# Moving gate products between attention and memory steps, with shared scaling, halved projections and split memory gates

## The chip, the cores and the metric

The kernel runs on one core of a Trainium2 chip. The metric is the device time of one execution in microseconds (us). Before the change it is 2273.91 us, the median of three runs (2273.75 to 2274.84). TensorE (PE in the rows) multiplies matrices into PSUM, which has eight banks of 128 x 512 fp32; VectorE (DVE), ScalarE (ACT) and GpSimd (POOL) do everything else; SyncE's queue (SP) issues most loads.

## The reference, cut to what matters

Two layers run over 256 latent tokens and 256 context tokens of width 1024, all in fp32: a half-step SwiGLU, three parallel token mixers, another half-step SwiGLU. The change is in the mixers alone:

```python
y_a = windowed_attention(qa, ka, va, ka_c, va_c, attn_sink)   # A: 8 heads, softmax with a sink
y_b = dense_attention(qb, concat(kb_c, kb), concat(vb_c, vb)) # B: 8 heads, normalised q and k
y_m, y_m_c = mlstm_mixer((qm, km, vm, om, gm), ...)           # C: bidirectional gated memory
...
z = einsum('btnw,nwd->btnd', stack([y_a, y_b, y_m], -2), w_branch)
g = sigmoid(gate_logits.reshape(..., 3, 1024))                # gate_logits = h @ w_in[gate columns]
return sum(g * z, axis=-2) @ w_out
```

In the second (last) layer only latent tokens are needed behind the keys and values, so queries, gates and merge there work on 256 tokens instead of 512.

## The kernel before

A product of fp32 values is made of three fp32r products, high x high, high x low and low x high (`mm3`, L192 to L196). Weights come as units of 128 x 1024 values (512 KB): SP loads one into a "raw" tile (L153, four of them), ACT rounds it to its high part (L163), DVE subtracts to get the low part (L164). A list of tasks, each with the units that it needs, is run in order (`run_tasks`, L168), and units are loaded and split a few tasks ahead. `weave(a, b)` spreads list b evenly through list a. Below the tasks, the framework's planner fixes each engine's order and hands out buffers of a ring as they come free, roughly in the order of the source, so that instructions of neighbouring tasks mix.

`mixer_tasks` (L830) lays out one layer's mixers in this order:

- Projections of branch A's queries, of values and keys; then the first of branch B's query projection `qb` (four tasks `tok_tasks`, L695: each multiplies two of the eight chunks of the inner dimension for all blocks of 128 tokens, 512 columns wide, so that one PSUM bank for each token block, four in all, is held from the first task to the last). The memory values `vm` are made in the same way. In the last layer `qb` is done ahead of the attention.
- Branch A's attention steps, the first half of `att` (16 steps in layer 0, 8 in layer 1), woven with `side`: the memory gates, the rest of `qb`, `vm`, and the queries' transposes; and with `pre_[0]`, gate products of branch 0. A gate product is 24 matmuls of 128 x W (W is 512 in layer 0, 256 in layer 1) into one bank (`gate`, L1299); `ahead` (L1306) copies it with ACT into half of a raw tile and, for each pair, writes it to memory, from where a unit "pre" brings it back for the merge.
- Branch B's steps and the last of A's (19 steps in layer 0, 11 in layer 1), woven with eight convolution tasks, each of which starts with such a product.
- Silu, then the memory steps (`mlstm_steps`), woven with the merge of branch 0 (`mrg[0]`) and gate products of branch 1 (`pre_[1]`); then the projection `om` woven with the merge of branch 1; `put_y2`, which transposes and splits the memory's result, three tasks into the rest of it; then the merge of branch 2 and the output projection.

`PRE = 8, 4, 0` and `PRE_L = 4, 4, 0` say how many of the eight gate products of each branch are made ahead in layer 0 and in layer 1. The others are made inside the merge task `mk` (L1316) itself, which multiplies the branch's result with its weights (12 matmuls), applies the sigmoid and adds up. For a pair that was made ahead, one sigmoid in place covers both halves of the loaded raw tile (L1328).

One attention step i takes two heads: scores into two banks (L1012 to L1015), row maximum (L1016), exponential with row sum (L1030), reciprocal (L1039), then POOL multiplies each head's probabilities with it in turn (L1042). Two steps later the probabilities are transposed into one or two banks (L1054) and split (L1056, through L189 and L190), and a step after that multiplied with the values (L1069, L1071).

The memory gates (`mgate_steps`, L1100) are three tasks: log-sigmoid; `rows`, which transposes them to rows and runs on DVE four scans (L1142), one long scan (L1144) and eleven more row operations (L1146 to L1153) in one task; and `cols`.

## Time and profile before

| | before |
|---|---|
| median of three runs | 2273.91 us |
| the profiled execution | 2271.84 us, of which the span is 2270.1 us |
| busy: TensorE, weight loads | 2195.6 us (97%), 1837.6 us (81%) |
| busy: DVE, ACT, POOL | 1545.9 us (68%), 984.6 us (43%), 133.0 us (6%) |
| mean granted TensorE clock | 0.992 |
| chain that ended last, by engine | PE 84%, DVE 8%, ACT 3%, DMA 2%, issue 2% |
| DMA | 331.36 MB, mean 146 GB/s |

TensorE is nearly always busy; the other engines have room on average, and so have the transfers. Layer 0's mixers run from about 440 to 950 us of the span, layer 1's from about 1750 to 2060 us. The two attention halves lie at 480 to 590 and 590 to 703 us in layer 0, at 1778 to 1840 and 1840 to 1903 us in layer 1; the memory steps at 715 to 781 and 1914 to 1967 us. A matmul's end is modelled, so that successive matmuls overlap in the rows; start times tell their pace.

### The profile page before, as it was taken

The page shows a single profiled execution, that of the slowest core. Times are in us where ns is not written, and L with a number is a line of the kernel's source. Part 1 is how long each engine was busy: PE and PEld are TensorE (multiplying, and loading weights), DVE is VectorE, ACT ScalarE, POOL GpSimd, SP SyncE. Part 2 cuts the span into 40 slices and gives each one's busy share as a digit, 9 for nine tenths or more (in the row PEclk, how much of TensorE's full clock was granted, in tenths as well). Part 3 has the DMA queues.
Part 4 walks back from the last instruction along what each step waited for, and adds up shares of the span by engine and source line. Part 5 has one row for each costly group of instructions (what it writes and reads, how often), then busy time and mean ns, then how long its engine had stood idle before and what let it go on. Part 6 is the DMA issues. An engine that isn't in the chain of part 4 may idle for free.

```text
span 2270.1 us, 30607 instructions
## 1 busy us (share of the span) xinstructions
PE 2195.6 (97%) x11666; PEld 1837.6 (81%) x11666; DVE 1545.9 (68%) x2756; ACT 984.6 (43%) x1569; POOL 133.0 (6%) x100
## 2 busy tenths in 40 slices
PE   6999999998999999999999999999999989998998
PEld 4877777787777888888878788777778878997997
DVE  3987775877678664654444378778849787786556
ACT  3322223554588533542222253222226488655444
POOL 0000000013241000000000000000000142000000
PEclk9999999999999999999999999999999999998999
DMA  7665564422213333434433336665634123565554
GB/s 282 214 196 186 165 199 149 125 81 76 94 38 82 119 119 136 142 115 135 129 114 127 103 107 204 195 195 178 223 116 159 57 89 96 167 228 172 189 186 153
DMA packets 126402, 331.36 MB, mean 146 GB/s; under 512 B 12712, under 2 KB 26088, under 8 KB 125488
## 3 DMA queue, kind: packets, MB, share of 16 engines
q1 hardware_dynamic: 111664, 314.02, 43.0%
q10 hardware_dynamic: 14592, 15.40, 2.2%
q8 instruction: 91, 1.49, 0.3%
q14 instruction: 55, 0.45, 0.1%
HBM read 320.91 MB, written 8.47 MB: 145 GB/s over the span
## 4 chain that ended last, share of the span: by engine, by line
PE 84%; DVE 8%; ACT 3%; DMA 2%; issue 2%; POOL 0%; ACTq 0%; POOLq 0%; SPq 0%; DVEq 0%
PE ps L194 26%; PE ps L195 26%; PE ps L196 26%; PE ps L1243 1%; DVE lo L164 1%; DVE sm L1016 1%; ACT t L1030 1%; PE ps L1212 1%; ACT hi L163 1%; PE ps L366 1%; PE ps L1054 1%; PE ps L468 1%; DVE t L190 0%; DVE slot L959 0%; DMA raw<-in_w_gu_dram 0%
## 5 line engine op out<-in xcount | busy, mean ns | idle before, releaser
L163 ACT ACTIVATE hi<-raw 128x1024 fp32r<-128x1024 f32 (+1 forms) x444 | 457.0, 1032 | 766.8 <-PE ps L195 274.7
L194 PE MATMUL ps<-slot,hi 128*128 128x512 f32 (+1 forms) x2232 | 780.5, 351 | 7.7 <-ACT slot L189 5.3
L195 PE MATMUL ps<-slot,hi 128*128 128x512 f32 (+1 forms) x2232 | 776.9, 349 | 0.9 <-DVE slot L190 0.7
L196 PE MATMUL ps<-slot,lo 128*128 128x512 f32 (+1 forms) x2232 | 776.6, 348 | 0.0
L164 DVE TENSOR_TENSOR lo<-raw,hi 128x1024 fp32r<-128x1024 f32 (+1 forms) x444 | 527.1, 1190 | 245.2 <-ACT hi L163 240.7
L194 PEld LDWEIGHTS ps<-slot,hi 128*128 128x128 f32 x2232 | 421.2, 190 | 77.5 <-ACT slot L189 6.6
L195 PEld LDWEIGHTS ps<-slot,hi 128*128 128x128 f32 x2232 | 422.5, 189 | 57.4 <-DVE slot L190 1.7
L196 PEld LDWEIGHTS ps<-slot,lo 128*128 128x128 f32 x2232 | 421.9, 189 | 57.9
L194 PE MATMUL ps<-hi,slot 128*128 128x512 f32 (+2 forms) x1048 | 400.6, 382 | 1.8 <-ACT slot L189 1.1
L196 PE MATMUL ps<-hi,slot 128*128 128x512 f32 (+2 forms) x1048 | 399.5, 382 | 0.0
L195 PE MATMUL ps<-lo,slot 128*128 128x512 f32 (+2 forms) x1048 | 399.5, 381 | 0.0
L358 DVE SCALAR_TENSOR_TENSOR t<-raw,sc,t 128x1024 f32<-128x1024 f32 x224 | 280.5, 1281 | 128.8 <-DMA raw<-in_w_ada_dram 128.5
L1042 POOL TENSOR_SCALAR t<-t,sm 128x512 f32<-128x512 f32 (+1 forms) x96 | 132.9, 1396 | 1767.1 <-DVE sm L1039 1675.7
L194 PEld LDWEIGHTS ps<-hi,slot 128*128 128x128 f32 x1048 | 197.5, 188 | 46.2 <-issue 5.7
L196 PEld LDWEIGHTS ps<-hi,slot 128*128 128x128 f32 x1048 | 197.0, 188 | 39.3
L195 PEld LDWEIGHTS ps<-lo,slot 128*128 128x128 f32 x1048 | 197.3, 188 | 38.8 <-issue 0.2
L189 ACT ACTIVATE slot<-t 128x512 fp32r<-128x512 f32 (+1 forms) x138 | 80.7, 594 | 185.4 <-DVE t L606 160.2
L606 DVE TENSOR_TENSOR t<-ps,t 128x512 f32<-128x512 f32 (+1 forms) x88 | 54.7, 622 | 89.1 <-PE ps L196 87.8
L190 DVE TENSOR_TENSOR slot<-t,slot 128x512 fp32r<-128x512 f32 (+1 forms) x138 | 87.6, 644 | 4.4 <-ACT slot L189 4.1
L1016 DVE TENSOR_REDUCE sm<-ps 128x1 f32<-128x512 f32 (+1 forms) x96 | 54.4, 593 | 22.2 <-PE ps L1015 21.5
L1054 PE MATMUL ps<-ident,t 128*128 128x128 f32 x320 | 47.7, 282 | 18.6 <-POOL t L1042 8.4
L1054 PEld LDWEIGHTS ps<-ident,t 128*128 128x128 f32 x320 | 37.5, 143 | 28.5 <-POOL t L1042 17.3
(198 smaller groups left out, 1670.6 us busy)
## 6 DMA issues: line engine op xcount, KB each, us to landing
raw<-in_w_gu_dram SPq DMA_DIRECT2D x176, 512.0 KB
raw<-in_w_ada_dram SPq DMA_DIRECT2D x128, 512.0 KB
raw<-in_w_down_dram SPq DMA_DIRECT2D x92, 512.0 KB
raw<-in_w_fm_dram SPq DMA_DIRECT2D x64, 512.0 KB
raw<-in_w_br_dram SPq DMA_DIRECT2D x24, 512.0 KB
raw<-in_w_out_dram SPq DMA_DIRECT2D x24, 512.0 KB
slot<-in_w_ada_dram SPq DMA_DIRECT2D x16, 512.0 KB
raw<-in_w_down_dram SPq DMA_DIRECT2D x20, 256.0 KB
```

The lines of the kernel that those rows point to most:

```text
L163: self.nc.scalar.activation(out=hi, in_=raw, func=AF.Copy)
L164: self.nc.vector.tensor_tensor(out=lo, in0=raw, in1=hi.bitcast(F32), op=ALU.subtract)
L189: self.nc.scalar.activation(out=hi, in_=src, func=AF.Copy)
L190: self.nc.vector.tensor_tensor(out=lo, in0=src, in1=hi.bitcast(F32), op=ALU.subtract)
L194: mm(out, lh, rh, start=start, stop=False, **kw)
L195: mm(out, lh, rl, start=False, stop=False, **kw)
L196: mm(out, ll, rh, start=False, stop=stop, **kw)
L358: v.scalar_tensor_tensor(out=acc, in0=units[0], scalar=c, in1=acc, op0=ALU.mult, op1=ALU.add)
L606: nc.vector.tensor_tensor(out=hid[:, :W], in0=ps[:, :W], in1=hid[:, :W], op=ALU.mult)
L1016: v.tensor_reduce(out=mx[:, e:e + 1], in_=ps[:, :nkey], axis=AX.X, op=ALU.max)
L1042: nc.gpsimd.tensor_scalar(out=t[:, :nkey], in0=t[:, :nkey], scalar1=r[:, e:e + 1], scalar2=None, op0=ALU.mult)
L1054: nc.tensor.transpose(pt[:, n * P:(n + 1) * P], e[n % 2][:, kb * P:(kb + 1) * P], self.ident)
```

## The change

Five things change together; what is computed stays the same.

1. All eight gate products of branches 0 and 1 are made ahead in both layers, those of branch 0 woven with branch A's steps, the first `PRE = 4` of branch 1 woven with the convolutions between branch B's steps, the other four in the memory steps. Of branch 2 the first `HELD = 2` stay in PSUM until their merge tasks; they stand behind the merge of branch 1, and `put_y2` comes right behind them.
2. Each merge task applies its own sigmoid into a new tile, ahead of its products, also where the logits were read back.
3. `qb` and `vm` become `half_tasks`: each unit has four of the eight inner chunks for half of the columns, so two tasks finish 256 columns for all token blocks, two blocks in one bank. The weights are laid out on the host so that a unit is one run of 4 KB for each partition.
4. The scaling of the probabilities is shared: POOL keeps the first head; the second goes to ACT in branch A and to DVE in branch B.
5. `rows` is cut into `rows`, `scans` and `decays`, and the first four gate tasks are woven with what is left of `qb`.

```diff
-PRE = 8, 4, 0
-PRE_L = 4, 4, 0
+PRE = 4
+HELD = 2
...
+    def half_tasks(self, l, name, tbs, ms, evac):
...
+        def mk(h, g):
+            def fn(units):
+                u = units[0]
+                for tb in tbs:
+                    if g == 0 and tb % 2 == 0:
+                        ds[h, tb // 2] = self.psum().rearrange("p (b c) -> p b c", b=2)
+                    ps = ds[h, tb // 2][:, tb % 2, :]
+                    for x in range(4):
+                        lh, ll = ms["hi"][g][:, x, tb * P:(tb + 1) * P], ms["lo"][g][:, x, tb * P:(tb + 1) * P]
+
+                        self.mm3(ps, lh, ll, u[0][:, x, :], u[1][:, x, :], g == x == tb % 2 == 0, g == 1 and x == 3,
+                                 skip_group_check=True)
+                    if g:
+                        evac(tb, h, ps)
+            return ([("half", l, name, h, g)], fn)
+
+        return [mk(h, g) for h in range(2) for g in range(2)]
...
-        side = gates[:1] + qb[:1] + gates[1:2] + qb[1:] + vm_[nv:va] + gates[2:] + vm_[va:vb] + qcols(1) + vm_[vb:]
+        side = weave(gates[:4], qb) + vm_[nv:va] + gates[4:] + vm_[va:vb] + qcols(1) + vm_[vb:]
         na = 4 * len(qtb)
-        out += weave(att[:na], weave(side, pre_[0])) + weave(att[na:], conv)
+        out += weave(att[:na], weave(side, pre_[0])) + weave(att[na:], weave(conv, pre_[1][:PRE]))
         out += self.silu_task(R, need_ctx)
         mem = self.mlstm_steps(R, qs)
-        out += mem[:1] + self.split_y(R, 0, W) + weave(weave(mrg[0], pre_[1]), mem[1:])
+        out += mem[:1] + self.split_y(R, 0, W) + weave(weave(mrg[0], pre_[1][PRE:]), mem[1:])
         out += self.split_y(R, 1, W)
-        out += weave(self.tok_tasks(l, "om", 512, 2, qtb, ms, om), mrg[1][:np_[1]])
-        out += mrg[1][np_[1]:np_[1] + 3] + [([], put_y2)] + mrg[1][np_[1] + 3:]
+        out += weave(self.tok_tasks(l, "om", 512, 2, qtb, ms, om), mrg[1][:2])
+        out += mrg[1][2:] + pre_[2] + [([], put_y2)]
         out += mrg[2]
...
             for e in range(2):
-                t = E[i][e]
-                nc.gpsimd.tensor_scalar(out=t[:, :nkey], in0=t[:, :nkey], scalar1=r[:, e:e + 1], scalar2=None,
-                                        op0=ALU.mult)
+                t = E[i][e][:, :nkey]
+                if e and x == 0:
+                    nc.scalar.activation(out=t, in_=t, func=AF.Copy, scale=r[:, e:e + 1])
+                else:
+                    (v if e else nc.gpsimd).tensor_scalar(out=t, in0=t, scalar1=r[:, e:e + 1], scalar2=None, op0=ALU.mult)
...
-            b_r, m_r = RW[:, 2, :], RW[:, 3, :]
-            i_r, f_r = RW[:, 0, :], RW[:, 1, :]
+            R["RW"] = RW
+
+        def scans(_):
+            RW = R["RW"]
+            i_r, f_r, b_r, m_r = (RW[:, q, :] for q in range(4))
...
+        def decays(_):
...
-        return [([], logsig), ([], rows), ([], cols)]
+        return [([], logsig), ([], rows), ([], scans), ([], decays), ([], cols)]
...
+        def held(j):
+            def fn(units):
+                st[j] = gate(units[0])
             return ([("fm", l, 8 + 8 * n + j)], fn)
...
-                if j >= npre:
-                    pg = gate(units.pop(0))
-                elif j % 2 == 0:
-                    st["g"] = units.pop(0).rearrange("p (a b) -> p a b", a=2)
-                    nc.scalar.activation(out=st["g"], in_=st["g"], func=AF.Sigmoid)
+                if n == 2:
+                    pg = gate(units.pop(0)) if j >= HELD else st.pop(j)
+                else:
+                    if j % 2 == 0:
+                        st["g"] = units.pop(0).rearrange("p (a b) -> p a b", a=2)
+                    pg = st["g"][:, j % 2, :]
+                g = self.t512()[:, :W]
+                nc.scalar.activation(out=g, in_=pg, func=AF.Sigmoid)
```

The row operations behind the halved `qb` (`q_rows`, L749) and the copies behind the halved `vm` work on 256 columns each, twice as often.

## Rows read from the trace of the kernel before

**Rows 1.** The page, busy time (share of the span) and instructions of an engine

```profile
PE 2195.6 (97%) x11666; PEld 1837.6 (81%) x11666; DVE 1545.9 (68%) x2756; ACT 984.6 (43%) x1569; POOL 133.0 (6%) x100
```

**Rows 2.** Stretches: length; PE, PEld, DVE, ACT, POOL busy; clock, DMA share, GB/s

```profile
480.00:590.00 110.00, 104.11 (x570) 85.18 (x569) 83.12 (x217) 57.59 (x127) 33.57 (x24) 1.00 0.19 64
590.00:703.00 113.00, 102.58 (x559) 85.70 (x558) 77.77 (x174) 80.63 (x157) 48.22 (x40) 0.98 0.28 84
1778.00:1840.00 62.00, 55.06 (x346) 45.63 (x344) 49.79 (x127) 33.44 (x73) 19.57 (x13) 0.97 0.19 64
1840.00:1903.00 63.00, 56.36 (x376) 49.91 (x375) 49.28 (x99) 52.10 (x90) 31.50 (x20) 0.97 0.22 73
715.00:781.00 66.00, 66.00 (x371) 57.59 (x370) 50.94 (x221) 46.08 (x91) 0.00 (x0) 1.00 0.28 89
1914.00:1967.00 53.00, 53.00 (x431) 52.09 (x431) 43.68 (x146) 46.56 (x89) 0.00 (x0) 1.00 0.41 135
1967.00:1999.00 32.00, 31.47 (x219) 28.92 (x219) 23.97 (x61) 15.01 (x19) 0.00 (x0) 1.00 0.68 223
```

**Rows 3.** TensorE's waits, 480 to 703 us: us in total, times, longest

```profile
PE ps L1054 <- POOL t L1042: 6.0, 8, 1.2
PE ps L1054 <- DVE t L190: 4.2, 2, 3.2
PE ps L1069 <- ACT t L1030: 2.0, 1, 2.0
...
PE ps L1012 <- ACT t L1030: 0.7, 1, 0.7
```

**Rows 4.** The same view, 1778 to 1903 us

```profile
PE ps L1054 <- DVE t L190: 2.9, 3, 1.2
PE ps L1054 <- POOL t L1042: 2.4, 3, 1.2
PE ps L1069 <- DVE t L190: 2.2, 2, 1.7
```

**Rows 5.** Timeline around 514 to 521 us: start us, length us, instruction, idle before it

```profile
514.66 1.35 DVE L1142 TENSOR_TENSOR_SCAN slot<-ones,slot 8x128 f32<-8x128 f32 x4
...
520.94 0.33 PE L1054 MATMUL ps<-ident,t 128*128 128x128 f32 x1 [3.16 <-DVE t L190]
```

**Rows 6.** Timeline of POOL, one step's pair of heads

```profile
618.52 3.10 POOL L1042 TENSOR_SCALAR t<-t,sm 128x512 f32<-128x512 f32 x2 [6.69 <-DVE sm L1039]
```

**Rows 7.** Groups by line and form: busy us, mean ns | idle before, releasers

```profile
L1042 POOL TENSOR_SCALAR t<-t,sm 128x512 f32<-128x512 f32 x64 | 102.7, 1616 | 1698.9 <-DVE sm L1039 1648.0 <-ACT t L189 18.1 <-ACT sm L1036 13.3
...
L451 DVE TENSOR_SCALAR t<-slot,sm 128x1024 f32<-128x1024 f32 x12 | 9.0, 753 | 0.4
...
L1341 ACT ACTIVATE t<-ps 128x512 f32<-128x512 f32 x12 | 7.0, 581 | 0.0
...
L163 ACT ACTIVATE hi<-raw 128x1024 fp32r<-128x1024 f32 x416 | 439.3, 1058 | 730.8 <-PE ps L195 266.4 <-PE ps L196 166.9 <-issue 154.2
...
L164 DVE TENSOR_TENSOR lo<-raw,hi 128x1024 fp32r<-128x1024 f32 x416 | 507.8, 1223 | 227.6 <-ACT hi L163 223.1 <-PE ps L196 1.4
...
L164 DVE TENSOR_TENSOR lo<-raw,hi 128x512 fp32r<-128x512 f32 x20 | 13.8, 689 | 16.4 <-ACT hi L163 16.4
```

**Rows 8.** Timeline of TensorE where the width of its matmuls changes

```profile
1914.05 0.40 PE L196 MATMUL ps<-slot,lo 128*128 128x512 f32 x1
1914.28 0.28 PE L194 MATMUL ps<-slot,hi 128*128 128x256 f32 x1
1914.40 0.28 PE L195 MATMUL ps<-slot,hi 128*128 128x256 f32 x1
```

**Rows 9.** Timeline of ACT, first and last of seven table loads, 1935 to 1962 us

```profile
1935.18 1.28 ACT L1341 ACT_TABLE_LOAD   x1
1936.47 0.39 ACT L1341 ACTIVATE t<-ps 128x256 f32<-128x256 f32 x1
...
1961.21 1.28 ACT L1341 ACT_TABLE_LOAD   x1
```

More of the change, by code (lines that the diff above doesn't have):

```diff
@@ L127, in unit_src @@
             return src.rearrange("(k p) c -> p k c", p=P), (len(ks), n), True
+        if kind == "half":
+            _, l, name, h, g = key
+            return a["w_" + name][l, h, g], (4, 256), True
         if kind == "fm":
@@ L909, in mixer_tasks @@
         kk_ = self.tok_tasks(l, "kk", 256, 4, range(4), ms, kk)
-        vm_ = self.tok_tasks(l, "vm", 512, 2, range(4), ms, vm)
+        vm_ = self.half_tasks(l, "vm", range(4), ms, vm)
         if need_ctx:
@@ L1144, in rows @@
             v.tensor_tensor_scan(out=m_r, data0=f_r, data1=i_r, initial=0.0, op0=ALU.add, op1=ALU.max)
+        def decays(_):
+            RW = R.pop("RW")
+            i_r, f_r, b_r, m_r = (RW[:, q, :] for q in range(4))
             KR = self.slot([8, 14, P])
@@ L1336, in fn @@
                              R[f"yl{n}"][:, k, :W], k == 0, k == 3)
-                if j < npre:
-                    g = st["g"][:, j % 2, :]
-                else:
-                    g = self.t512()[:, :W]
-                    nc.scalar.activation(out=g, in_=pg, func=AF.Sigmoid)
                 u = R["u"][j // 4][:, j % 4, :]
@@ L1353, in mk @@
             return (keys, fn)
-        return [ahead(j) for j in range(npre)], [mk(j) for j in range(8)]
+        first = [held(j) for j in range(HELD)] if n == 2 else [ahead(j) for j in range(8)]
+        return first, [mk(j) for j in range(8)]
 def weave(a, b, head=0, tail=0):
@@ L1446, in _layout @@
     a["w_qa"] = c(w[:, :, C_QA + qcols])
-    a["w_qb"] = c(w[:, :, C_QB + qcols])
+    halves = lambda m: c(m.reshape(2, 2, 4, P, 2, 256).transpose(0, 4, 1, 3, 2, 5))
+    a["w_qb"] = halves(w[:, :, C_QB + qcols])
     a["w_kk"] = c(np.concatenate([w[:, :, C_KA:C_KA + 128], w[:, :, C_KB:C_KB + 128]], axis=2))
```

47 lines of the change are left out of this document (26 added, 21 removed).

## The prediction

> **What bounds the kernel now.** I read the page's busy times first. TensorE is busy for 2195.6 of 2270.1 us [rows 1], so only its own stream can move the time: either its idle time shrinks, or its work changes. The change adds and removes almost no products, so the question is where TensorE idles, and whether the changed order fills those holes or opens others. The second view is the table of stretches [rows 2]. Its first four rows are the two attention halves of layer 0 and of layer 1: TensorE is missing 110.00-104.11=5.9, 113.00-102.58=10.4, 62.00-55.06=6.9 and 63.00-56.36=6.6 us there, 29.9 us together. In the memory steps of both layers, the next two rows, it is missing nothing, and in the start of layer 1's merge, the last row, 0.5 us. So what can be won lies in the attention, and what can be lost lies in stretches that are full today.
>
> Two things make a hole dearer than its idle time. Matmuls of 512 columns start 0.23 us apart while each is drawn 0.40 us long [rows 8], so the drawn end covers about 0.16 us of each hole. And the granted clock averages 0.98, 0.97 and 0.97 in three of the four stretches [rows 2], that is 0.02x113+0.03x62+0.03x63=6 us of clock, lost in falls to the lower of its two levels (1.2 instead of 2.4 GHz); part of each fall lies in holes, so I count 4 us of it as TensorE time. The view of waits has about 34 of them in these stretches, 5.4 us at 0.16. The ceiling of any gain is therefore about 29.9+5.4+4=39 us, 1.7%.
>
> The third view, who TensorE waited for, splits the 29.9. In layer 0: POOL's probability scaling L1042, 6.0 us in 8 waits; DVE's L190, 4.2 us; and the exponentials L1030 (four rows from 2.0 down to 0.7, 5.2 us together), which is PSUM not yet free [rows 3]. In layer 1: DVE's L190 2.9+2.2, POOL 2.4 [rows 4]. The rest, some 7 us, is scattered.
>
> **The change, part by part.**
>
> *Scaling shared.* POOL scales both heads of a step now, one after the other: 3.10 us for a pair [rows 6]. Afterwards the second head goes to ACT in branch A and to DVE in branch B. The trace has no DVE scaling of 512 columns from SBUF; one of 1024 took 0.753 [rows 7], so half of that, 0.38, and all of it bound the price, and I take 0.4, since a shorter operation cannot be near the full one. ACT's copy of 512 I take from the sigmoid of that size, 0.58 [rows 7]. So the transposes, which wait for both heads, can start about 1.5 us earlier in a 512-column step. The added load is 16x0.4=6 us on DVE in layer 0's branch B, busy there for 77.77 of 113, and 16x0.58=9 us on ACT in branch A, busy for 57.59 of 110 [rows 2]: beside TensorE's work in both. ACT keeps its order, so a scaling that waits for DVE's reciprocal holds the exponentials and weight splits queued behind it, and through them PSUM banks; with half of ACT free in branch A I price that at nothing (up to a reciprocal's delay of some 0.5 us a step, 12 us, if that cover is gone). Of the 8.4 us of POOL waits I take 6.7 as won (0 to 8.4).
>
> POOL's mean for 512 columns is 1616 ns [rows 7], above half of the undisturbed pair in [rows 6]: it slows at times. The Trainium skill (GPSIMD Engine Reference, Key points) says that POOL and DVE share their SBUF interfaces and contend when DVE runs in a two-port mode or with two SBUF inputs; by it the new DVE scaling would run against POOL's half. The trace agrees in that the mean exceeds the pair's half; were POOL's single scaling to take 2 us, the pair's end would still come 1.1 us earlier and the sum would lose about 2 us.
>
> *Projections halved, memory gates split.* qb and vm run as half-width products, and an output block holds two PSUM banks over two tasks instead of four over four. Four of the eight banks are held through most of the first attention halves now; hence the waits for L1030 and for L190, which empty banks. The gate rows run on DVE as one block: from 514.66 on DVE works at the scans and what follows them, and TensorE, whose next transposes wait for L190 behind that block, stands 3.16 us until 520.94 [rows 5]. As three tasks with other work between, the block should fall into pieces of about half. Of L190's 4.2+2.9+2.2=9.3 us and L1030's 5.2 I take 6.8 and 3.4, about seven tenths (0 to 14.5). Cost on TensorE: two matmuls of 256 columns at 0.12 replace one at 0.23 [rows 8], 0 to 0.01 us more; for 336 of them (96 qb and 96 vm in layer 0, 48 and 96 in layer 1) that is 0 to 3.4 us, all on the path; I take 1.5. Cost on DVE: two operations of half the width cost 2x0.689-1.223=0.155 more than one [rows 7]; 14 operations on qb's rows in layer 0 make 2.2 us beside 110 us of TensorE.
>
> *Gate products moved.* Layer 0: four gates (24 products of 512, 5.6 us each) come between branch B's steps as filler and leave the merge. Layer 1: eight gates (24 of 256, 2.9 us each) move ahead, four into each attention half. In layer 0's branch B that is 22 us of work on top of 102.6 for the same 19 steps, so each step's chain of maximum, exponential, scaling and transposes has a fifth more cover. A gate brings ACT 1.05 and DVE 1.22 for its weights [rows 7] and ACT an evacuation of 0.58; ACT would then be busy for about 87 and DVE for 89 of some 130 us: a smaller share than now. The scattered holes I leave as they are.
>
> Sum of the gain: 6.7+6.8+3.4=16.9 us of idle time, some 22 waits x0.16=3.5, and about half of the clock's loss, 2.2: 22.6 us.
>
> *What loses cover.* In layer 1's memory steps [rows 2] four gates leave, 4x24x0.12=11.5 us: TensorE's work there falls from 53.0 to 41.5 us. ACT's falls less: 46.56-4x1.05=42.4, and eight single sigmoids replace four (+1.3), each a possible change of ACT's table at 1.28 us [rows 9]. So ACT has 43.7 or more against 41.5, and the memory products wait for its exponentials. I take 4 us lost (0 to 13.7, worked out below). DVE, at 43.68-4x1.22=38.8, stays just under. Layer 0's memory steps keep their twelve tasks; ACT at 46.08 of 66 [rows 2] has room for four more sigmoids there and their table changes, 12 us at most: hidden, and 0 to 3 lost if they come in a bunch.
>
> In the trace the next activation starts 0.01 us behind the 1.28 of a table load [rows 9]. The Trainium skill (ScalarE: Activation LUTs, What ACT_TABLE_LOAD costs) gives about 2.66 us for a switch with its drain, and its rule is to finish one table set before the next, which speaks against one sigmoid per task. By its figure seven loads would cost 9.7 us more and ACT would not fit into this stretch, where it does fit, so the trace does not bear the price out; the rule is the last rival below.
>
> *Merge.* In layer 1 the last six tasks of branch 1 keep 12x0.12=1.44 us of products each and read 512+256 KB per pair: 0.79 MB in 2.88 us, 273 GB/s. The start of the merge moved 223 GB/s at a DMA share of 0.68 [rows 2], so 273 is a share of 0.83. DVE needs 1.22 for weights and four operations of 256 columns at 0.42 (by the slope of the two L164 rows [rows 7]), 2.9 us per pair. Both just fit: 1 us lost (0 to 3). put_y2 now stands right before the products that read it. Its eight DVE operations of 512 columns in layer 0, 8x0.69=5.5 us, are covered only by an independent gate (5.6 us) issued ahead of those products; in layer 1 it is 2.8 against 2.9. I take 1 us (0 to 8). The extra writes and reads of logits, about 2 MB in each layer, lie in stretches with DMA shares of 0.19 to 0.41 [rows 2]: nothing.
>
> Sum: 22.6-1.5-4-1-1=15.1 us. The profiled execution took 2271.84 (span 2270.1 and 1.7 around it): 2256.7. The median of the runs, 2273.91, stands 2.1 above it, so I forecast 2259 us; its own range is 2246 to 2268.
>
> **The rivals.** *A clean attention.* If filler, banks and shared scaling close all holes, the 39 us come in, less about 2 for the halves and the merge: 2273.9-37=2237. For it: where filler is plenty, as in the memory steps, there are no holes today. Against it: the waits have four different releasers. *Waits that only change their name.* ACT is the busiest helper in the second halves, 80.63 of 113 and 52.10 of 63 [rows 2]; if it comes last where POOL did, only some 7 us come in and the costs eat them: 2274, no change. That the gate steps end up back to back in DVE's order after all, so that the change doesn't do what it says, belongs here. *Table changes bind ACT (slower).* Sigmoids of logits that were read back come one per task, among exponentials. If each of the eight in layer 1's memory steps flips the table twice, 16 loads replace seven [rows 9]: ACT has 43.7+9x1.28=55.2 against TensorE's 41.5, 13.7 us lost; the same flips among branch B's exponentials undo the gain there. Then only the first halves win, some 10 us, against 1.5+13.7+2: 2281. It decides once the flips cost the 15 us that the forecast leaves, six more than today, each 2.56. Against it: the two sigmoids of a pair wait for one load from memory and can share a table.
>
> **How the numbers follow.** Forecast 0.60, clean 0.15, no change 0.13, slower 0.12. A range of 2240 to 2279 leaves out most of the clean case and most of the slower one. 0.2% (4.5 us) is about what a measurement of this kernel can tell from no change. Faster 0.75, same 0.13, slower 0.12.
>
> **What would show it.** Right: POOL busy for about half of what it is now; less than 15 us missing in the four stretches together; no wait of 3 us behind the gate rows; ACT nearly full in layer 1's memory steps, with a few us of holes on TensorE. Wrong: POOL's waits replaced by equal ones for ACT; holes of over 8 us in layer 1's memory steps or behind put_y2; a dozen more table loads.

## The result, and the profile after

The changed kernel is slower: 2284.93 us, the median of four runs (2281.97 to 2289.74), against 2273.83 in the same comparison; ratio 1.0052, 95% interval 1.0040 to 1.0064. The forecast of 2259 us, faster, had the wrong sign and was 26 us off, and the time lies above the range (2240 to 2279). The profiled execution took 2281.97 us, its span 2280.2, 10.1 more than before.

The page's busy times after the change [rows 1]: TensorE does 336 products more and is idle longer, POOL is down to about half.

```profile
PE 2197.1 (96%) x12002; PEld 1855.0 (81%) x12002; DVE 1558.5 (68%) x2808; ACT 1004.4 (44%) x1629; POOL 71.1 (3%) x52
```

The stretches that answer to [rows 2], in the same columns (length; PE, PEld, DVE, ACT, POOL busy; clock, DMA share, GB/s). The lines are in order: the first and second attention half of layer 0, those of layer 1, then layer 0's merge up to put_y2, layer 1's memory steps, and layer 1's merge up to put_y2. The bounds are shifted, since work has moved.

```profile
480.00:593.00 113.00, 102.64 (x683) 90.43 (x682) 81.38 (x232) 64.12 (x146) 17.33 (x13) 0.95 0.22 68
593.00:732.00 139.00, 134.65 (x759) 115.09 (x758) 102.20 (x216) 99.93 (x189) 24.83 (x19) 1.00 0.27 87
1790.00:1847.00 57.00, 50.02 (x392) 46.22 (x391) 47.84 (x118) 35.04 (x77) 11.70 (x7) 0.97 0.23 75
1847.00:1941.00 94.00, 93.99 (x675) 87.26 (x674) 73.31 (x140) 73.73 (x127) 17.05 (x10) 1.00 0.38 119
...
802.00:862.00 60.00, 56.57 (x245) 45.48 (x244) 36.22 (x92) 20.73 (x27) 0.00 (x0) 0.97 0.40 132
1941.00:1975.00 34.00, 34.00 (x267) 32.99 (x266) 30.56 (x121) 32.82 (x70) 0.00 (x0) 1.00 0.33 109
1975.00:2017.00 42.00, 34.18 (x222) 31.19 (x221) 31.42 (x77) 18.55 (x28) 0.00 (x0) 0.88 0.59 193
```

The second attention halves are what was hoped for: 4.4 us missing in 139 and nothing in 94, where 10.4 and 6.6 were missing in 113 and 63 [rows 2]. The first halves got no better: 10.4 and 7.0 us are missing, where it was 5.9 and 6.9, and the clock of layer 0's fell to 0.95. And the merges, full before, now have holes: 3.4 us in layer 0, 7.8 in layer 1 with a clock of 0.88.

A balance by stage, from the start times of marks in the timeline of TensorE (first score, first memory score, first transpose of the stage behind the merge). The projections are counted from a transpose of the normalised inputs, in layer 0 from the first one, in layer 1 from the last one; from the first, layer 1's take 66.1 and 69.0 us, and the row's result becomes -9.8:

| us | before | after | work moved in or out | so lost (+) or won (-) |
|---|---|---|---|---|
| layer 0, projections and attention | 66.7 + 231.1 | 64.9 + 250.5 | +22.3 (4 gates) | -4.7 |
| layer 0, memory steps and merge | 241.1 | 230.5 | -22.3 | +11.7 |
| layer 1, projections and attention | 36.1 + 135.2 | 39.4 + 145.2 | +22.7 (8 gates) | -9.4 |
| layer 1, memory steps and merge | 145.4 | 135.1 | -22.7 | +12.4 |

A gate is 24 products at 0.232 us (W 512) or 0.118 (W 256). The sum, +10.0, is the 10.1 us of the span. So the attention won 14 us (with the cost of the halves in it), and the merges lost 24.

**The first halves.** TensorE's waits, 480 to 593 us (us in total, times, longest), and then those from 1790 to 1847:

```profile
PE ps L1163 <- DVE s L1153: 5.7, 1, 5.7
PE ps L1163 <- DVE s L1152: 3.0, 1, 3.0
PE ps L1038 <- DVE slot L810: 1.5, 1, 1.5
```

```profile
PE ps L1038 <- DVE slot L810: 3.7, 1, 3.7
PE ps L1163 <- DVE s L1153: 3.0, 1, 3.0
```

L1163 are the small transposes that make the gate rows, L1152 and L1153 the copies that end the gate task `logsig`. L1038 is the first score, L810 the split of the query columns. DVE's timeline shows why the rows wait so long. The log-sigmoid begins at 488.69, behind the column splits and row maxima, and its last copy ends at 499.08:

```profile
488.69 0.22 DVE L1134 TENSOR_TENSOR s<-gm,gateb 128x64 f32<-128x64 f32 x1
...
493.73 0.16 DVE L1139 TENSOR_SCALAR s<-s 128x32 f32<-128x32 f32 x1
...
496.14 1.55 DVE L1145 SCALAR_TENSOR_TENSOR s<-s,s 128x32 f32<-128x32 f32 x7
...
498.40 0.68 DVE L1153 COPY s<-s 128x16 f32<-128x16 f32 x2
```

The new order `weave(gates[:4], qb)` puts its first filler behind the second gate task, so in layer 0 `rows` follows directly on the log-sigmoid that it needs; in the kernel before, a task of `qb` stood between. That explains layer 0 alone: in layer 1 no task of `qb` is left by then in either kernel, and what makes its rows wait 3.0 us, where they waited 0.3 at most before, stays open; with half a task of `vm` between (the first experiment below) that wait is gone. During the waits the clock of layer 0 fell to its lower level, 1.2 GHz, for 10 us:

```profile
491.70:502.00 10.30, 4.60 (x23) 2.38 (x21) 5.74 (x27) 4.18 (x13) 3.12 (x2) 0.50 0.29 95
502.00:590.00 88.00, 87.79 (x587) 79.01 (x586) 62.66 (x182) 52.06 (x122) 14.20 (x11) 1.00 0.23 74
```

**The merges.** ACT's timeline at the start of layer 1's merge, and the product that waits for it:

```profile
1994.97 1.02 ACT L1371 ACTIVATE t<-raw 128x256 f32<-128x256 f32 x3
1998.18 0.42 ACT L1371 ACTIVATE t<-raw 128x256 f32<-128x256 f32 x1 [2.19 <-DVE t L1314]
1998.78 0.42 ACT L1371 ACTIVATE t<-raw 128x256 f32<-128x256 f32 x1 [0.18 <-DVE sm L1310]
2002.19 0.42 ACT L1371 ACTIVATE t<-raw 128x256 f32<-128x256 f32 x1 [3.00 <-DVE t L1314]
2003.19 0.42 ACT L1371 ACTIVATE t<-raw 128x256 f32<-128x256 f32 x1 [0.58 <-DVE slot L1385]
2003.51 2.93 ACT L166 ACTIVATE hi<-raw 128x1024 fp32r<-128x1024 f32 x3
...
2004.61 0.58 PE L197 MATMUL ps<-slot,hi 128*128 128x256 f32 x1 [6.36 <-ACT hi L166]
```

The new single sigmoids (L1371) wait for L1314, the memory's read-out on DVE. They don't need its values; what they can be waiting for is its temporary: both take their tiles from the one ring of eight 512-column temporaries, of which the results y stay occupied until put_y2. The split of the branch weights (L166) stands behind the sigmoids on ACT, and TensorE behind it: 6.4 us. Layer 0 has the same hole at 838 us, 3.1 us. The others in the merges are 3.7 and 1.7 us behind put_y2, where the product waits for the split of what put_y2 transposed.

### The profile page after: what moved, and what is told of

Same layout as the page of the kernel before. It is cut to its first block, busy times and chain, and to the rows that moved or that the text cites. A ratio compares the mean times of both kernels' runs of the same rounds, so it can differ in the third digit from the quotient of the medians.

```text
span 2280.2 us, 31311 instructions
## 1 busy us (share of the span) xinstructions
PE 2197.1 (96%) x12002; PEld 1855.0 (81%) x12002; DVE 1558.5 (68%) x2808; ACT 1004.4 (44%) x1629; POOL 71.1 (3%) x52
## 4 chain that ended last, share of the span: by engine, by line
PE 85%; DVE 7%; ACT 4%; DMA 3%; issue 1%; ACTq 0%; DVEq 0%
PE ps L197 26%; PE ps L198 26%; PE ps L199 26%; DVE lo L167 1%; PE ps L1082 1%; ACT hi L166 1%; PE ps L1278 1%; PE ps L1097 1%; PE ps L369 1%; PE ps L1038 1%; PE ps L1099 1%; PE ps L1041 1%; PE ps L471 1%; DVE slot L193 1%; ACT t L1260 1%
## 5 line engine op out<-in xcount | busy, mean ns | idle before, releaser
L166 ACT ACTIVATE hi<-raw 128x1024 fp32r<-128x1024 f32 (+1 forms) x444 | 457.1, 1032 | 775.0 <-PE ps L198 263.4
L197 PE MATMUL ps<-hi,slot 128*128 128x512 f32 (+2 forms) x1160 | 420.0, 362 | 4.1 <-DVE slot L810 1.8
L198 PE MATMUL ps<-lo,slot 128*128 128x512 f32 (+2 forms) x1160 | 416.8, 360 | 0.4 <-DVE lo L167 0.4
L199 PE MATMUL ps<-hi,slot 128*128 128x512 f32 (+2 forms) x1160 | 416.6, 360 | 0.0
L197 PEld LDWEIGHTS ps<-hi,slot 128*128 128x128 f32 x1160 | 218.0, 188 | 46.6 <-issue 7.0
L198 PEld LDWEIGHTS ps<-lo,slot 128*128 128x128 f32 x1160 | 218.1, 188 | 35.8 <-DVE lo L167 0.9
L199 PEld LDWEIGHTS ps<-hi,slot 128*128 128x128 f32 x1160 | 217.6, 188 | 35.9 <-DVE slot L193 0.2
L1071 POOL TENSOR_SCALAR t<-t,sm 128x512 f32<-128x512 f32 (+1 forms) x48 | 70.9, 1477 | 1844.3 <-DVE s L1153 1090.6
L606 ACT ACTIVATE t<-ps 128x512 f32<-128x512 f32 (+1 forms) x88 | 46.5, 528 | 23.6 <-DVE t L429 16.5
L193 DVE TENSOR_TENSOR t<-ps,t 128x512 fp32r<-128x512 f32 x80 | 53.8, 680 | 0.7 <-ACT t L192 0.6
```

The costliest lines, as they stand in the source:

```text
L166: self.nc.scalar.activation(out=hi, in_=raw, func=AF.Copy)
L193: self.nc.vector.tensor_tensor(out=lo, in0=src, in1=hi.bitcast(F32), op=ALU.subtract)
L197: mm(out, lh, rh, start=start, stop=False, **kw)
L198: mm(out, lh, rl, start=False, stop=False, **kw)
L199: mm(out, ll, rh, start=False, stop=stop, **kw)
L606: nc.scalar.activation(out=hs["sg"][:, :W], in_=ps[:, :W], func=AF.Silu)
```

## The experiments

Line numbers of an experiment can stand one to five lines off those of the kernel that it was made from. All ratios are to the kernel before, with a 95% interval.

**Mending one order of the changed kernel at a time.**

```diff
+        gap, nv = (qb[:1], nv) if qb else (vm_[nv:nv + 1], nv + 1)
-        side = weave(gates[:4], qb) + vm_[nv:va] + ...
+        side = gates[:1] + gap + weave(gates[1:4], qb[1:]) + vm_[nv:va] + ...
```

> The changed kernel, with one projection task put between the gates' log-sigmoid and the matrix products of the gate rows (in layer 0 the first half of qb that is left, in layer 1 a half of vm); nothing else moves. Theory (the rows stand right behind their own log-sigmoid in TensorE's order, so TensorE waits out DVE's chain): the holes of 3.2 and 6.0 us of layer 0 and of 3.2 us in layer 1 go, and so does most of the 10 us at half clock that follow in layer 0; 2285 falls by 9 to 14 us, to about 2273. Rival (DVE is late there anyway with column splits, maxima and weight splits, and whatever stands next waits as long): the holes only move by one task, 2282 to 2286.

2279.72 us, 1.0029 (1.0018 to 1.0040): 5 us won, halfway. The two waits of the rows are gone, and in their place the first transposes of probabilities wait, in this kernel's view of waits from 475 to 590 us:

```profile
PE ps L1083 <- POOL t L1072: 5.5, 1, 5.5
PE ps L1039 <- DVE slot L810: 1.5, 1, 1.5
```

So the theory was half right: DVE is late at this place whatever stands next, and one task more between is not enough. What had been lacking showed when filler was put ahead of the first scores too:

```diff
-QC = 1
-VA, VB = 1, 2
-VL = 1, 1, 2
+QC = 2
+VA, VB = 2, 4
+VL = 2, 2, 4
...
-        side = weave(gates[:4], qb) + vm_[nv:va] + ...
+        side = gates[:1] + qb + gates[1:4] + vm_[nv:va] + ...
```

> The changed kernel with more projection products ahead of the attention and none lost: two halves of qb instead of one (layer 0) and two halves of vm instead of one (layer 1) stand before the first scores, and the two qb halves that are left stand between the log-sigmoid and the gate rows. With the task alone put between them, the hole of 5.6 us at 488 and the holes of 1.6 and 4.6 us ahead of the first scores stayed. Theory (at the start of each attention DVE still splits the query columns, some 6 us of it, and TensorE has too little to do until then): the three holes and the half clock behind them go, minus 10 to 15 us against the changed kernel, about 2272. Rival (the filler is only missing later, since the sum of it is the same): holes of like size appear further down the first halves, 2280 or more.

2268.64 us, 0.9979 (0.9971 to 0.9988): 16 us less than the changed kernel. Layer 0 lost its holes at the start but for one of 1.6 us for POOL and one of 1.8 for ACT. Layer 1 did not gain: its wait for the query columns grew from 3.7 to 4.6 us. So the same was tried in layer 0 alone, with `VL` as it was:

> The changed kernel with the added cover in layer 0 alone (two halves of qb ahead of the first scores, two between log-sigmoid and rows); layer 1 as changed. Theory (layer 0's order is the whole gain of the run with cover in both layers, and layer 1's cost about 4 us there): 2264 to 2268. Rival (layer 1's order brought part of it): 2272 or more.

2269.71 us, 0.9983 (0.9974 to 0.9992), the same within the intervals: layer 0's order is the gain. The stretch from the projections to the memory steps takes 69.6 + 234.4 us there, 11.4 less than in the changed kernel; by the ratios the whole is 15 us. Most of the rest, 3.7 us, stands between layer 0's merge and layer 1's mixers (760.3 us instead of 764.0), where no order was changed and the products only follow one another a little faster; why stays open, so 11 us are what the order is shown to be worth.

The merges were asked in the same way. The read-back sigmoid in place on the pair:

```diff
+                        nc.scalar.activation(out=st["g"], in_=st["g"], func=AF.Sigmoid)
-                    pg = st["g"][:, j % 2, :]
-                g = self.t512()[:, :W]
-                nc.scalar.activation(out=g, in_=pg, func=AF.Sigmoid)
+                    g = st["g"][:, j % 2, :]
+                if n == 2:
+                    g = self.t512()[:, :W]
+                    nc.scalar.activation(out=g, in_=pg, func=AF.Sigmoid)
```

> The changed kernel, with the sigmoid of logits that were read back done in place, on both gates of a pair at once, as in the kernel before, instead of singly into a fresh temporary of 512 columns. Theory (the ring of eight such temporaries is short while the read-out's results wait for put_y2, so the sigmoid waits for the read-out and holds ACT's weight splits behind it): the holes of 3.2 us (837.9) and 6.5 us (1998.0) at the start of the two merges go with part of the half-rate clock that follows, minus 8 to 14 us, about 2274. Rival (the weight units themselves come late, since the merge has lost its filler and must load and split branch weights faster): the holes stay, 2282 to 2286.

2273.67 us, 1.0001 (0.9992 to 1.0010): 11 us won. Layer 0's hole is gone, layer 1's shrank from 6.4 to 2.9 us. Whether it is the ring or the weights' transfers was asked with a tile from elsewhere:

```diff
+                        if n == 1:
+                            st["g"] = self.t1024()[:, :2 * W].rearrange("p (a b) -> p a b", a=2)
+                            nc.scalar.activation(out=st["g"], in_=raw, func=AF.Sigmoid)
```

> The changed kernel with branch 1's read-back logits put through one sigmoid per pair into a tile of the 1024-column ring, which is idle after the memory steps; put_y2 stays behind the held gates. Theory (the 512-column ring is what the sigmoid waits for): the holes of 3.2 us at the start of layer 0's merge and of 6.5 us at the start of layer 1's go, or shrink at least as much as with the sigmoid in place (to 0 and 3 us), 2271 to 2276. Rival (it is the raw buffers, the weights' transfers or the number of sigmoids): the holes stay within 1 us of what they are, 2282 to 2286.

2275.97 us, 1.0007 (0.9998 to 1.0016): the holes at the start of both merges are gone altogether. This run, like the one in place, has fewer sigmoids too, but the order and number of the transfers are the changed kernel's, and the waits for L1314 went with the ring; that sigmoid count alone would do it isn't excluded by a run of its own. Next, TensorE in layer 1 waits 5.0 us at put_y2, for the read-out. DVE's timeline of this kernel ahead of that:

```profile
2005.06 0.15 DVE L221 TENSOR_TENSOR sm<-sm 128x4 f32<-128x4 f32 x1
2005.13 1.22 DVE L167 TENSOR_TENSOR lo<-raw,hi 128x1024 fp32r<-128x1024 f32 x1
2006.27 0.15 DVE L222 TENSOR_TENSOR sm<-sm,sm 128x4 f32<-128x4 f32 x1
2006.34 1.22 DVE L167 TENSOR_TENSOR lo<-raw,hi 128x1024 fp32r<-128x1024 f32 x1
2007.47 0.15 DVE L223 SCALAR_TENSOR_TENSOR sm<-sm,sm 128x4 f32<-128x4 f32 x1
2007.66 1.14 DVE L1314 SCALAR_TENSOR_TENSOR t<-slot,sm,t 128x128 f32<-128x128 f32 x4
```

The read-out's reciprocal root is a chain of small operations, 0.15 us each, and a weight split of 1.22 us stands in front of nearly every one: a step of the chain takes 1.2 us.

put_y2 again three tasks behind the projection `om`. That is not quite its old place: in the kernel before, seven of branch 1's eight merge tasks stood ahead of it, four of them woven with `om`, and here it is five, with two woven:

```diff
-        out += mrg[1][2:] + pre_[2] + [([], put_y2)]
+        out += mrg[1][2:5] + [([], put_y2)] + mrg[1][5:] + pre_[2]
```

> The changed kernel, with put_y2 back in front of the last three tasks of branch 1 (five tasks stand ahead of it, as in the kernel before) and the two held gates behind those. Theory (put_y2's split has only two gates' products as cover): the holes of 3.9 and 0.5 us behind it in layer 0 and of 1.9 us in layer 1 go with the half clock behind the first, minus 5 to 9 us, about 2278. Rival (its transposes and splits now meet the merge's weight splits on ACT and DVE and make the same hole elsewhere): within 2 us of 2285.

2273.30 us, 0.9997 (0.9988 to 1.0005): 12 us won, more than expected: the first hole of layer 0's merge goes too. That it goes because put_y2 gives the temporaries back earlier fits, but is argued. In layer 1 put_y2 now waits 3.6 us for the read-out. All three edits together:

> The changed kernel with the three edits together: a task between log-sigmoid and gate rows, the read-back sigmoid in place on the pair, put_y2 in front of the last three tasks of branch 1. Theory (three separate holes): their gains add, 12+11+7, to about 2255, some 19 us below the kernel before. Rival (the gates' products are the merge's only slack, so that whichever wait is removed, the weight supply is late next): at most half of it, 2270 or more.

2276.86 us, 1.0011 (1.0002 to 1.0020): no better than either merge edit alone, so the theory of three separate holes fell for the merge. ACT's timeline in layer 0, and put_y2's transposes:

```profile
822.45 0.60 ACT L920 ACTIVATE t<-ps 128x512 f32<-128x512 f32 x1 [0.26 <-PE ps L199]
...
831.90 1.06 ACT L166 ACTIVATE hi<-raw 128x1024 fp32r<-128x1024 f32 x1 [8.34 <-DMA raw<-in_w_br_dram]
832.87 0.57 ACT L920 ACTIVATE t<-ps 128x512 f32<-128x512 f32 x1
...
843.27 1.17 PE L1009 MATMUL ps<-ident,t 128*128 128x128 f32 x4 [5.11 <-DVE t L1315]
```

The fourth block's sigmoid of `om` (L920, 832.87), with which its read-out begins, stands on ACT behind a weight split that waits 8.3 us for its transfer, and put_y2, now early, finds the read-out unfinished. By the code the sigmoids in place hold the load buffers until their products are read; that this made the transfer late is argued, not shown. The pair's sigmoid in the other ring, with put_y2 early, does not help that:

> The changed kernel with put_y2 in front of the last three tasks of branch 1, and with branch 1's read-back logits put through one sigmoid per pair into a tile of the 1024-column ring, which is idle after the memory steps; so the sigmoid takes neither a 512-column temporary nor holds its input buffer. Theory (the read-out is late because both rings run short: the 512 ring when the sigmoid takes from it, the raw ring of weight loads when it is done in place): the waits for the read-out ahead of put_y2 (2.9 and 0.7 us in layer 1 with put_y2 moved alone, 5.3 and 1.4 in layer 0 with both edits) go, about 2268. Rival (branch 1 has lost its gates' products and DVE's and ACT's work on weights, products and read-out simply takes longer than TensorE's): holes of 5 us or more stay ahead of put_y2 or behind it, 2273 or more.

2282.20 us, 1.0038 (1.0025 to 1.0052). The rival held: put_y2 waits 6.1 us for the read-out in layer 0 and 4.6 and 4.3 in layer 1. Why the two edits together take longer than either alone isn't shown.

**One part alone.** The shared scaling, on the kernel before (the diff is the change's):

> The kernel before with the shared scaling alone: the second head goes to ACT in branch A and to DVE in branch B. By the prediction's first term (POOL's waits of 8.4 us, with what their drawn ends hide, 6.7 won): minus 7 to 9 us, about 2266. Rival (the waits only change their name, ACT or DVE being late where POOL was): 2272 to 2276.

2276.86 us, 1.0018 (1.0008 to 1.0027): slower. Its waits from 480 to 703 us against [rows 3]:

```profile
PE ps L1056 <- DVE t L190: 5.7, 3, 3.1
PE ps L1056 <- POOL t L1045: 3.9, 4, 1.5
PE ps L1071 <- DVE t L190: 2.1, 2, 1.4
PE ps L1071 <- ACT t L1030: 1.9, 1, 1.9
PE ps L194 <- DVE slot L959: 1.5, 1, 1.5
```

POOL is waited for 3.9 us instead of 6.0, but DVE, which got the second head in branch B, 5.7 instead of 4.2 by the transposes, 2.1 by the products with the values (L1071) and 1.5 at the convolution (L959). The waits changed their name, as the prediction's second rival had it, though to DVE and not to ACT. The halves:

```diff
-        qb = self.tok_tasks(l, "qb", 512, 2, qtb, ms, qq(1))
+        qb = self.half_tasks(l, "qb", qtb, ms, qqb)
...
-        vm_ = self.tok_tasks(l, "vm", 512, 2, range(4), ms, vm)
+        vm_ = self.half_tasks(l, "vm", range(4), ms, vm)
```

> The kernel before with the halved projections qb and vm alone; scaling, gate steps and gate products stay. By the prediction's terms (waits for L1030, 3.4 of 5.2 us, won with the banks; 336 small products more, 1.5 us lost): minus 1 to 3 us, about 2272. Rival (in the first halves the holes at the start, 1.6 us ahead of the first scores in layer 0 and 4.4 in layer 1, come with the halves, since the query columns of both halves are ready no earlier and the filler ahead of the first scores is cut): plus 4 to 8 us, about 2280.

2278.21 us, 1.0023 (1.0013 to 1.0034): slower, with the waits ahead of the first scores that the rival named (1.5 and 4.4 us) and 6.3 us for POOL at the first transposes. The gate steps in five tasks, order kept:

```diff
-        side = gates[:1] + qb[:1] + gates[1:2] + qb[1:] + vm_[nv:va] + gates[2:] + ...
+        side = gates[:1] + qb[:1] + weave(gates[1:4], qb[1:]) + vm_[nv:va] + gates[4:] + ...
```

> The kernel before with its gate steps in five tasks instead of three, alone, and with one projection task kept between the log-sigmoid and the rows, as it was. By the prediction's term (the block behind which transposes waited falls into pieces): the hole of 3.2 us at 517 goes, minus 3 to 6 us with the drawn ends, about 2269. Rival (DVE's total is unchanged and its backlog only shifts): within 2 us of 2274.

2269.69 us, 0.9981 (0.9972 to 0.9990): 4 us faster, the size forecast. The 3.16 us of [rows 5] are gone, the longest wait of the transposes for L190 there is 0.6, but the longest for an exponential is 2.8 instead of 2.0, and layer 0's attention takes 234.0 us instead of 231.1. The gain is layer 1's, 128.8 instead of 135.2. These three together, in the changed kernel's order (no gate product moved):

> The changed kernel without its third part: the gate products of the branches, their sigmoids and put_y2 stand where the kernel before has them; shared scaling, halved projections and the gate steps in five tasks stay. Theory (the moved gates close branch B's holes but cost some 12 us in each merge): the merges are as before, the first attention halves have the changed kernel's holes at the start (about 12 us), branch B keeps about half of its 10 us: 2274 to 2282. Rival (the whole loss is the moved gates'): 2262 to 2268.

2289.19 us, 1.0070 (1.0056 to 1.0084). The parts alone sum to +0.22%; 0.48% or 11 us are left. This kernel has the 3.0 and 5.7 us waits of the rows, and its layer 0 takes 64.9 + 240.7 us up to the memory steps, 7.8 more than before; 4.8 more are in layer 1's memory steps and merge, where put_y2 waits 3.0 us for the read-out. With the gates back in it, layer 0's merge has no wait at all. And the moved gates alone:

> The kernel before with the moved gate products alone: all eight of branches 0 and 1 made ahead, two of branch 2 held, single sigmoids, put_y2 behind them; projections, scaling and gate steps stay. Theory (branch B gains what the changed kernel gained there, some 6 us in layer 0 and 9 in layer 1, and the merges lose 11.7 and 12.4 us as there): 2274+24-15, about 2283, or 2278 if branch B gains more with free banks. Rival (by the difference of the changed kernel and the one without its moved gates, 0.52% against 0.70%, moving them gains): about 2270.

2279.28 us, 1.0026 (1.0016 to 1.0036): slower, between the two values expected. Its second halves are nearly clean, and its merges have the holes shown above (3.0, 3.7, 6.4, 1.6 us). Counted as in the balance, its memory steps and merges lose 11.8 and 13.5 us: the loss there comes with the first two parts of the change alone.

**The mended kernel.** Layer 0 as in the run with cover in layer 0 alone; put_y2 early in layer 0 only, the sigmoid in place in layer 1 only, so that the two merge edits don't meet:

```diff
+        if need_ctx:
+            out += mrg[1][2:5] + [([], put_y2)] + mrg[1][5:] + pre_[2]
+        else:
+            out += mrg[1][2:] + pre_[2] + [([], put_y2)]
...
+                        if len(qs) == 1:
+                            nc.scalar.activation(out=st["g"], in_=st["g"], func=AF.Sigmoid)
```

> The changed kernel with three orders mended: in layer 0 two halves of qb ahead of the first scores and two between log-sigmoid and rows (layer 1 as changed), put_y2 in front of the last three tasks of branch 1 in layer 0 alone, the read-back sigmoid in place on the pair in layer 1 alone. Theory (the losses are three separate orders, and the two merge edits do not add only because both would meet in one merge): 11.5 from layer 0's attention, 8.6 from its merge, 6.1 from layer 1's merge, taken from the changed kernel's 2284: about 2258, 0.7% below the kernel before. Rival (what is late only moves on, as when the edits stood together): 2265 to 2272.

2256.37 us (2254.83 to 2257.99), 0.9925 (0.9912 to 0.9939): 17 us faster than the kernel before, with all five parts of the change in it. Its stretches: both attention halves of layer 0, both of layer 1, the two merges up to put_y2.

```profile
483.00:583.00 100.00, 96.73 (x646) 86.64 (x645) 74.77 (x220) 60.61 (x138) 16.55 (x12) 0.98 0.22 70
583.00:714.00 131.00, 128.14 (x740) 110.22 (x740) 100.43 (x215) 94.37 (x186) 25.83 (x20) 1.00 0.27 85
1771.00:1824.00 53.00, 46.91 (x340) 41.76 (x341) 41.52 (x105) 30.53 (x67) 11.42 (x6) 0.90 0.22 70
1824.00:1919.00 95.00, 95.00 (x686) 88.36 (x685) 76.28 (x147) 75.34 (x135) 17.27 (x10) 1.00 0.35 112
783.00:828.00 45.00, 45.00 (x210) 36.82 (x208) 27.09 (x102) 12.87 (x18) 0.00 (x0) 1.00 0.31 104
1951.00:1989.00 38.00, 34.48 (x234) 32.03 (x234) 27.91 (x91) 18.84 (x25) 0.00 (x0) 0.96 0.52 168
```

Layer 0's merge has no hole up to put_y2, and layer 1's half of what the changed kernel had. The first half of layer 1, whose order was left, still misses 6.1 us, with waits of 3.7 us ahead of the first score and 3.0 for the gate rows. Counted as in the balance, against the kernel before, the attention of both layers wins 21.5 us (14.8 and 6.7) and the merges lose 8.8 (2.8 and 6.0); 2.6 us are won between the layers' mixers, where nothing was changed. In this setting single parts were undone again. Scaling back on POOL alone:

> The same mended kernel with the shared scaling undone: POOL scales both heads of a step again, in both branches. Theory (the shared scaling was worth nothing alone, since DVE or ACT came last in POOL's place, and costs the busier engines time): 0 to 5 us faster than the mended kernel. Rival (with filler in branch B the pair on POOL would again be waited for, 8.4 us as in the kernel before): 5 to 9 us slower than it.

2258.59 us, 0.9932 (0.9920 to 0.9944): neither expectation; the difference of 2 us can't be told from none. Whole projections in place of the halves (`QC`, `VA`, `VB` as before):

> The mended kernel with whole projections in place of the halves, in the order of the kernel before (one projection task ahead of the attention, one between log-sigmoid and rows, the others between the gate steps); moved gates, shared scaling, five gate tasks, put_y2 early in layer 0 and the in-place sigmoid in layer 1 stay. Theory (the halves cost by their order: with the whole ones the holes of 1.6 and 3.9 us ahead of the first scores and of 3.4 us behind log-sigmoid in layer 1 go, with 336 small products): 2246 to 2251. Rival (halves free banks early, and without them branch A waits for banks again): 2256 or more.

2264.04 us, 0.9959 (0.9947 to 0.9972): 8 us slower, as the rival had it. The halves can't be credited with all of it, though: 3.6 of the 7.7 us between the two profiled spans stand in the stretch between the layers' mixers (764.0 us instead of 760.4), where nothing differs. And the order was undone with them: one projection task stands ahead of the attention instead of two, and layer 1's gate rows wait 7.0 us. So with filler in the right places the halves and their order are worth 4 to 8 us; alone, without it, the halves cost 5. And both undone:

> The same with the shared scaling undone too (POOL scales both heads): of the five parts the moved gates and the split gate steps stay. Theory (sharing costs DVE and ACT what it spares POOL): within 3 us of the one with shared scaling. Rival (POOL's pair of 3.1 us is waited for in branch A, where no gates were added for layer 0): 4 to 8 us slower.

2265.18 us, 0.9968 (0.9956 to 0.9980): within the 3 us expected. Last, layer 1's pairs in the other ring:

> The mended kernel, whose layer 1 sends branch 1's pairs through one sigmoid into a tile of the idle 1024-column ring, instead of doing it in place in the load buffer. Theory (in place the load buffers are held until the products are read, so the branch weights come late, the hole of 3.2 us left at 1977): that hole goes, 2252 to 2255. Rival (the weights are late for their transfers alone, or the read-out sets the end): 2255 to 2259.

2257.52 us, 0.9933 (0.9919 to 0.9946), the same as the mended kernel: the hole of 3.0 us for the weight split goes, and put_y2 waits 4.3 us for the read-out instead. That wait, and one of 1.4 us behind it, are what is left in layer 1's merge up to put_y2's products.

## Why the prediction was wrong

**Which view bounds it.** Right: TensorE's idle time decides, what can be won lies in the attention, and what can be lost lies in stretches that were full. The four rows of the balance above sum to the measured difference.

**Merge, 1 us, and put_y2, 1 us (0 to 8).** This is the term that failed: 24 us for the two layers. The prediction weighed sums in layer 1's merge, DMA share and DVE's load per pair, and found that both just fit; the start of layer 0's merge, which loses 22 us of gates, it didn't price at all. It did not follow the chains. The gates' products, 22 us in layer 0's merge and 11 in layer 1's (the other 11 left the memory steps), had stood beside the read-out, the sigmoids and put_y2's split; without them each of these came last in turn. With the gates left in place, layer 0's merge has no wait, and with the moved gates alone, their single sigmoids and put_y2's place included, both merges have the same holes. The single sigmoid's new tile was costed only as a possible table change; that it takes from a ring which the read-out occupies, ahead of the weight splits in ACT's order, wasn't looked at. The runs with another tile, in place, and with put_y2 moved show this, and that the chains lie close behind one another. In the mended kernel, with the gates still gone, the merges lose 8.8 us, so some 15 of the 24 were these orders. What the rest hangs on isn't separated: in layer 1 the wait only moves, from the weight split (3.0 us) to the read-out (4.3), when the sigmoid's tile changes.

**Gate steps split, part of 6.8 us.** Alone its size was about right (4 us), but by another way: the wait at 517 went, yet layer 0's attention took 2.9 us longer, and the gain came in layer 1. The step that failed was "as three tasks with other work between": for the first pair the new order has nothing between in layer 0, and the rows waited 8.7 us there, with 10 us at the lower clock; of the marks, "no wait of 3 us behind the gate rows" failed. Steps back to back stood in the prediction under the rival of no change, at no loss. Mended in layer 0, that order and its filler are worth 11 us.

**Halves, 1.5 us cost, 3.4 of bank waits won.** The 336 products came as counted. Alone the halves lost 5 us, in the mended kernel they and their order won 4 to 8; the term wasn't a constant but hung on the filler around it, which the prediction didn't ask. Why the filler ahead of the first scores does less with halves, though a task is as long, stays open: in the kernel before 33 products stand between the query transposes and the first score, nine of them of a later task; in the changed one only the 48 half ones of the task itself.

**Scaling shared, 6.7 us.** Wrong: POOL's busy time halved as said, but alone it lost 4 us, and in the mended kernel it won nothing measurable. The prices were low as well:

```profile
L1071 POOL TENSOR_SCALAR t<-t,sm 128x512 f32<-128x512 f32 x32 | 55.7, 1742 | 1751.4 <-DVE s L1153 1090.6 <-DVE sm L1065 617.4 <-ACT t L1106 16.4
...
L1071 DVE TENSOR_SCALAR t<-t,sm 128x512 f32<-128x512 f32 x16 | 8.6, 535 | 0.4
...
L1069 ACT ACTIVATE t<-t,sm 128x512 f32<-128x512 f32 x16 | 11.5, 721 | 8.1 <-DVE sm L1065 7.4 <-DVE s L1153 0.6
```

DVE takes 0.54 us (0.65 with the sharing alone; 0.4 assumed), ACT 0.72 (0.58 assumed), and POOL's single one 1.74 on the mean, where it was 1.62 [rows 7]. That rise does not come with the sharing alone: POOL's mean is 1.58 with the sharing alone, and 1.72 with the moved gates alone, when POOL scales both heads. In the changed kernel's second halves half of them take 1.56 to 1.57 us, and the longest has a weight split of DVE beside it:

```profile
666.66 2.44 POOL L1071 TENSOR_SCALAR t<-t,sm 128x512 f32<-128x512 f32 x1 [4.17 <-DVE sm L1065]
```

```profile
666.39 1.21 DVE L167 TENSOR_TENSOR lo<-raw,hi 128x1024 fp32r<-128x1024 f32 x1
```

The two overlap for 0.94 us, and the scaling takes 0.88 longer than an undisturbed one. This agrees with what the Trainium skill (GPSIMD Engine Reference, Key points) says: POOL shares its SBUF interfaces with DVE and contends with DVE instructions that have two SBUF inputs, as the split has. That the moved gates' splits are the whole rise isn't shown.

**Gates moved into branch B.** Right: the second halves miss 4.4 us and none, and no wait of over 1.8 us stands there.

**Memory steps of layer 1, 4 us (0 to 13.7).** Did not come: TensorE was busy for 34.00 of 34.00 us, with ACT at 32.82. ACT came as close to full as forecast but was nowhere last. The tables were loaded 41 times, 43 before, at 1.28 us, so the slower rival's mechanism did not act here. The rule of the Trainium skill (ScalarE: Activation LUTs, Rules for kernel authors), to do all of one table set before switching, was not put to the test: all runs here have 39 to 43 loads.

**The sum.** Of the 26 us, about 7 are attention (21.1 net forecast, 14.1 measured), 22 the merges (2 forecast, 24.1 measured), less the 4 of the memory steps; 1 is the median, which stands 3.0 above the profiled execution instead of 2.1. That the mended kernel's attention wins 21.5 us, close to the 21.1, is luck in part: the shared scaling, 6.7 of the forecast, gave nothing measurable there. The slower side had a rival with the wrong mechanism; the one that came true, chains that lose their cover in the merge, was there as two terms of 1 us with a range of 11, and stood under no rival.

## What to carry to other kernels

Independent products that stand in a full stage may be what hides its dependent chains: before they are moved to a stage with holes, each chain that stays behind is to be walked through with the cover that it has left, down to the ring that each new tile comes from and to what stands behind its waiting instruction on an in-order engine. A step cut into tasks helps only where something else stands between the tasks, also between the first two. And parts of a change are to be measured with the order around them mended, since the same part can lose 5 us in one order and win in another.

## What the runs showed of the hardware

A hole can cost more than its length. TensorE stood idle for 3.0 us at 487, did 16 small transposes and stood for 5.7 more; over 10.3 us from 491.7 its granted clock was 0.5 (1.2 GHz), and pairs of the small transposes began 0.43 us apart there, 0.22 before. In layer 1's merge a fall of the same length began inside the hole of 6.4 us:

```profile
2000.40:2010.70 10.30, 5.11 (x22) 4.82 (x23) 8.88 (x21) 4.73 (x6) 0.00 (x0) 0.50 0.56 179
```

ACT's price shows the source and the operands. For 128 x 512 values the sigmoid took 0.628 us from SBUF and 0.581 from PSUM. The exponential from PSUM took 0.687 with one value for each partition (its bias) and 0.775 with two (bias and scale); the copy from SBUF with such a scale took 0.721.
